# Hyena filter parts made in the feed-forward layer, sums of squares on DVE: one change to a two-layer encoder

## The chip, the core and the metric

The kernel runs on one core of a Trainium2 chip. The metric is the device time of one execution in microseconds (us); three runs of the kernel before took 1322.36, 1323.95 and 1324.27 us, a median of 1323.95. PE is the matrix engine, PEld its weight loads, DVE the vector engine, ACT the scalar engine, POOL the GpSimd engine, SP the engine that only issues DMAs.

## What is computed

Two layers of an encoder over 512 tokens of width 1024. Each layer is a mixer and a convolutional feed-forward block, and each of the four sub-layers is wrapped as `x = x + post_norm(f(pre_norm(x)))` with RMS norms over the width. The mixer of layer 0 joins latent attention and neighbourhood attention; the mixer of layer 1 joins retention and a Hyena operator. What the change touches is the filter of the Hyena operator and the norms:

```python
def rms_norm(x, gain):
    y = x * lax.rsqrt(jnp.mean(x * x, axis=-1, keepdims=True) + EPS)
    return y * gain

def hyena_filters(...):                      # 512 positions, hidden 64, 2 x 512 channels
    h = jnp.sin(freq * (z @ w1 + b1))
    h = jnp.sin(freq * (h @ w2 + b2))
    h = jnp.sin(freq * (h @ w3 + b3))
    h = h @ w4
    return h[:, :512] * window, h[:, 512:] * window

def hyena_operator(...):
    x0, x1, v = split(dwconv3(u_proj, short_conv), 3)
    u = v * x1
    y = irfft(rfft(u, n=1024) * rfft(k_circ, n=1024))[:512] + u * hy_bias
    return y * x0
```

The filter depends on weights alone, not on x.

## The kernel before

Activations lie transposed, width on the partitions: x and the normalised input h are eight tiles of 128x512 (k = 0 to 7). Every large product is made of three fp32r products of parts: `split_to` (line 273) writes hi = fp32r(src) on ACT and lo = src - hi on DVE, and `mm` (line 278) adds hi*hi, hi*lo and lo*hi (lines 280, 281 and 282). Weights are handled the same way in `load_weight` (line 250): the SP queue loads 512 KB into one of two raw buffers, ACT casts it (line 259), DVE subtracts (line 260), three weights ahead of use. PSUM has eight banks under four tags: pj (2), A (3), B (2), C (1).

All instructions are written in one program order; a scheduler orders each engine's instructions ahead of time, by data, buffers and a priority that follows the program, which `high_priority` moves forward and `issue_after` holds back. Each engine, and each queue of DMA issues, then works in that order. A buffer of a phase lies over buffers of the phase before it and waits until those are free.

**The boundary** (line 339) joins a sub-layer to the next one. It makes the last output tiles in two halves of 256 tokens (ca, cb); `evac` squares each; `stats` (line 286) sums over the partitions by products with a column of ones (line 292), a POOL power gives the factor (line 299), `spread` (line 311) makes it a row by transposes (line 316). `update` (line 388) then multiplies f by the factor (line 392), adds the residual x (line 393) and makes h in two parts (`scaled`: ACT line 333, DVE line 334), half by half. `squares` (line 399) squares the new x on ACT (line 406), into the no longer needed old x tiles, and POOL adds them into acc2 (line 407). Meanwhile `proj_halves` (line 455) has PE make the first four products of the next sub-layer, half by half, from weights of which all four are held to the end. Since the new factor is applied after the products, its statistics are needed only then: those of the first half are put behind the third of four product groups, those of the second half behind the fourth (lines 437 to 445). They give rcol and its row Rb.

**The feed-forward block** (line 867) makes 22 pairs of products; each takes PE 2 x 24 products, and DVE and ACT do the rest (lines 894 to 912). In layer 0, at every second pair, one step of `filters` (line 963) runs beside it: three hidden layers (line 975, fp32) with a range-reduced sine, then four token blocks, each with two fp32 products with w4 (line 986), windows, a sum and a difference on POOL (line 989) and their stores of 256 KB (line 990).

**The mixer of layer 1** (line 1047) first writes the eight x tiles to memory (line 1051, ACT's queue) and loads the two DFT constants of 1 MB on POOL's queue (line 934). The four products that the boundary left in PSUM become u: scale by Rb (line 1061), short convolution (lines 1063 to 1065). Products for x1 and x0 follow, between them eight steps of `spectrum` (line 994): a filter tile is loaded (line 1003, ACT's queue), split, and multiplied by the DFT constants into the one bank of tag C. The scale tile cv is a single buffer. `decays` (line 1026) is a chain of some 25 small DVE instructions and one exponential.

Of the kernel before, what the change touches and what calls it, by code (L numbers as in the profile page):

```python
# [16 lines left out]
P = 128  # L17
S = 512
# [187 lines left out]
class Body:  # L206
    def __init__(self, ctx, tc, I, out, dbg=None):
# [10 lines left out]
        self.filt = self.dp.tile([2, S, HC], F32, name="filt")  # L218
# [120 lines left out]
    def boundary(self, pool, tag, x, prod, gpost, gpre, ns, ftag, perm=False, rin=None):  # L339
# [85 lines left out]
        if not last:  # L425
            with self.tc.issue_after(self.pow.ins):
                squares(ca)
# [439 lines left out]
    def ffn(self, p, x, h, pre, l):  # L867
# [15 lines left out]
        if l == 0:  # L883
            new = lambda n, tag, bufs: p.tile([P, S], F32, tag=tag, bufs=bufs, name=self.nm(n))
            room = [new("fa", "s", 3) for _ in range(3)] + [new("fb", "flt", 2) for _ in range(2)]
            steps = self.filters(room + [self.X("fc") for _ in range(2)])

        for j in range(FT):
# [5 lines left out]
            nc.vector.tensor_tensor(t, gps, Rb, ALU.mult)  # L894
# [68 lines left out]
    def filters(self, room):  # L963
        nc = self.nc
        z, fw, w4f, w4b, fh, a, n = room
        w4 = (w4f, w4b)
        nc.sync.dma_start(z[:33], self.I["fz"])
        nc.sync.dma_start(fw[:64, :192], self.I["fw"][:64, :192])
        for d in range(2):
            nc.sync.dma_start(w4[d][:64], self.I["fw"][:64, 192 + d * HC:192 + (d + 1) * HC])  # L970
        yield
        k = 33
        for i in range(3):
# [4 lines left out]
            yield  # L978
        for tk in range(4):
            par, hh = tk // 2, tk % 2  # L980
            lhs = z[:64].rearrange("p (m two) -> p two m", two=2)[:, par, hh * P:hh * P + P]
            win = (a, n)
            for d in range(2):
                nc.sync.dma_start(win[d], self.I["fwin"][:, (tk * 2 + d) * HC:(tk * 2 + d + 1) * HC])
                ps = self.PS("C")
                nc.tensor.matmul(ps, lhs, w4[d][:64], start=True, stop=True)
                nc.vector.tensor_tensor(win[d], ps, win[d], ALU.mult)
            for i, (t, op) in enumerate(((fh, ALU.add), (fw, ALU.subtract))):
                nc.gpsimd.tensor_tensor(t, a, n, op)
                nc.sync.dma_start(self.filt[i, tk * P:(tk + 1) * P], t)  # L990
# [3 lines left out]
    def spectrum(self, mats, at, kt, spec):  # L994
        nc = self.nc
        for par in range(2):
            for trig in range(2):
                m = 2 * par + trig
                sd = []
                for hh in range(2):  # L1000
                    t = self.X("sd", tag="xb")
                    tk = 2 * par + hh
                    nc.scalar.dma_start(t, self.filt[trig, tk * P:(tk + 1) * P])
                    sd.append(at(trig))
                    self.split_to(*sd[-1], t)
                for ft in range(2):
                    ps = self.PS("C")
                    for hh in range(2):
                        c = slice(ft * P, ft * P + P)
                        self.mm(ps, (mats[0][:, m, hh, c], mats[1][:, m, hh, c]), sd[hh], hh == 0, hh == 1)  # L1010
                    if par == 0:
                        t = self.X("sp", tag="xb")
# [270 lines left out]
```

## Time and profile before

| | us |
|---|---|
| median of three runs | 1323.95 |
| the profiled execution, its own time | 1324.02 |
| its span, first to last instruction | 1321.9 |
| PE busy | 1282.6 |
| DVE busy | 809.0 |
| ACT busy | 583.1 |
| POOL busy | 132.5 |

Layer 0's mixer ends near 255 us, the first boundary lies at 255 to 300, layer 0's feed-forward block at 300 to 640, the second boundary and the start of layer 1's mixer at 640 to 720, the third boundary at 935 to 980, layer 1's feed-forward block behind it. Times in the trace count from the span's start. In a timeline a row gives start, duration, engine, line, operation, output and inputs, shape and count, and in brackets how long the engine stood idle before it and for whom. A matmul's duration is its own way through the array; what it costs PE is the distance to the next start.

### The profile page before, as it was taken

Reading aid. Unit: us, or ns where it says so; the run is one execution under the profiler, and the core shown is the slowest. Engines: PE = TensorE matmul, PEld = TensorE weight load, DVE = VectorE, ACT = ScalarE, POOL = GpSimd, SP = SyncE. Lnnn points to the kernel's source line nnn. Section 1 sums busy time; section 2 is a strip of 40 time slices with the busy share of each in tenths; the row PEclk is TensorE's granted clock in tenths of the full one; section 3 lists DMA queues with packets and bytes.
Section 4 is the critical chain, followed back from the end, with each engine's and each line's share of the span. In section 5 each row is a group of like instructions: output and inputs, shape, how many; then the busy total and the mean of one; then the engine's idle time right before and its main releaser. Section 6 shows DMA issues by size and latency. Waiting matters only on the chain.

```text
span 1321.9 us, 16451 instructions
## 1 busy us (share of the span) xinstructions
PE 1282.6 (97%) x6370; PEld 1062.2 (80%) x6370; DVE 809.0 (61%) x1269; ACT 583.1 (44%) x943; POOL 132.5 (10%) x126
## 2 busy tenths in 40 slices
PE   8999799999999999999889999999999999999997
PEld 7788677997877788888887878778988888888886
DVE  7679897479756555222668795775775555553223
ACT  5355798456523333222444234544553333332221
POOL 4021322040011000000230000000210000000002
PEclk9999899999999999999989999999999999999999
DMA  7222012223434322333253233213233333333331
GB/s 269 81 64 80 1 32 81 80 70 118 119 121 144 112 96 96 103 105 103 73 207 127 64 114 107 72 57 115 79 96 100 98 101 101 96 96 97 111 96 64
DMA packets 41402, 130.35 MB, mean 99 GB/s; under 512 B 4619, under 2 KB 6859, under 8 KB 40812
## 3 DMA queue, kind: packets, MB, share of 16 engines
q1 hardware_dynamic: 35708, 116.66, 27.6%
q10 hardware_dynamic: 5040, 8.45, 1.9%
q0 software_dynamic: 576, 4.19, 0.8%
q8 instruction: 50, 0.82, 0.3%
q14 instruction: 28, 0.23, 0.1%
HBM read 122.99 MB, written 6.29 MB: 98 GB/s over the span
## 4 chain that ended last, share of the span: by engine, by line
PE 84%; DVE 7%; ACT 3%; issue 2%; DMA 2%; POOL 1%; SPq 0%; DVEq 0%; ACTq 0%; POOLq 0%
PE pspj L280 16%; PE pspj L282 16%; PE pspj L281 16%; PE psA L280 9%; PE psA L282 9%; PE psA L281 9%; DVE wlo L260 2%; DVE f L393 1%; DVE h L334 1%; ACT e L792 1%; DVE f L392 1%; DMA raw<-in_w 1%; PE psB L292 1%; PE psB L669 1%; PE psB L808 1%
## 5 line engine op out<-in xcount | busy, mean ns | idle before, releaser
L259 ACT CAST whi<-raw 128x1024 fp32r<-128x1024 f32 (+1 forms) x200 | 209.2, 1048 | 437.7 <-PE pspj L281 243.0
L260 DVE TENSOR_TENSOR wlo<-raw,whi 128x1024 fp32r<-128x1024 f32 (+1 forms) x200 | 247.6, 1240 | 215.2 <-ACT whi L259 212.8
L280 PE MATMUL pspj<-h,whi 128*128 128x512 f32 (+1 forms) x664 | 251.8, 379 | 2.4 <-DVE v L597 2.3
L281 PE MATMUL pspj<-h,whi 128*128 128x512 f32 (+1 forms) x664 | 250.9, 378 | 1.4 <-DVE h L334 1.4
L282 PE MATMUL pspj<-h,wlo 128*128 128x512 f32 (+1 forms) x664 | 251.2, 378 | 0.0
L282 PE MATMUL psA<-h,wlo 128*128 128x512 f32 (+1 forms) x424 | 156.3, 369 | 4.4 <-DVE wlo L260 4.3
L280 PE MATMUL psA<-h,whi 128*128 128x512 f32 (+1 forms) x424 | 157.6, 372 | 0.0
L281 PE MATMUL psA<-h,whi 128*128 128x512 f32 (+1 forms) x424 | 155.8, 367 | 0.0
L280 PEld LDWEIGHTS pspj<-h,whi 128*128 128x128 f32 x664 | 126.5, 191 | 25.2 <-DVE v L597 2.7
L281 PEld LDWEIGHTS pspj<-h,whi 128*128 128x128 f32 x664 | 126.5, 191 | 24.0 <-DVE h L334 1.8
L282 PEld LDWEIGHTS pspj<-h,wlo 128*128 128x128 f32 x664 | 126.5, 190 | 22.5 <-issue 0.2
L280 PE MATMUL pspj<-ahi,whi 128*128 128x512 f32 x308 | 121.4, 394 | 0.0
L282 PE MATMUL pspj<-ahi,wlo 128*128 128x512 f32 x308 | 120.7, 392 | 0.0
L281 PE MATMUL pspj<-alo,whi 128*128 128x512 f32 x308 | 119.5, 388 | 0.0
L280 PEld LDWEIGHTS psA<-h,whi 128*128 128x128 f32 x424 | 81.0, 191 | 19.8 <-issue 5.4
L282 PEld LDWEIGHTS psA<-h,wlo 128*128 128x128 f32 x424 | 80.8, 191 | 19.4 <-DVE wlo L260 6.3
L281 PEld LDWEIGHTS psA<-h,whi 128*128 128x128 f32 x424 | 80.9, 191 | 12.2
L299 POOL TENSOR_TENSOR r<-v,mhalf 128x2 f32<-128x2 f32 (+1 forms) x14 | 13.7, 982 | 702.1 <-DVE v L297 543.0
L894 DVE TENSOR_TENSOR t<-psA,Rb 128x512 f32<-128x512 f32 x40 | 27.6, 690 | 87.8 <-PE psA L282 87.7
L282 PEld LDWEIGHTS pspj<-ahi,wlo 128*128 128x128 f32 x308 | 57.8, 188 | 13.6
L281 PEld LDWEIGHTS pspj<-alo,whi 128*128 128x128 f32 x308 | 57.8, 188 | 12.9
L280 PEld LDWEIGHTS pspj<-ahi,whi 128*128 128x128 f32 x308 | 57.9, 188 | 11.5
(357 smaller groups left out, 2188.4 us busy)
## 6 DMA issues: line engine op xcount, KB each, us to landing
raw<-in_w SPq DMA_DIRECT2D x198, 512.0 KB, 3.5
x<-in_xT SPq DMA_DIRECT2D x16, 256.0 KB, 4.2
fc<-in_fwin SPq DMA_DIRECT2D x8, 256.0 KB, 4.0
filt<-fa SPq DMA_DIRECT2D x8, 256.0 KB, 2.0
xspill<-f ACTq DMA_DIRECT2D x8, 256.0 KB, 2.2
sd<-filt ACTq DMA_DIRECT2D x8, 256.0 KB, 3.4
x<-xspill ACTq DMA_DIRECT2D x8, 256.0 KB, 3.0
rpb<-in_rpb SPq DMA_DIRECT2D x4, 384.0 KB, 4.8
```

The lines of the kernel that those rows point to most:

```text
L259: nc.scalar.copy(hi[:, c], raw[:, c])
L260: nc.vector.tensor_tensor(lo[:, c], raw[:, c], hi[:, c].bitcast(F32), ALU.subtract)
L280: nc.tensor.matmul(ps, stat[0], mov[0], start=start, stop=False)
L281: nc.tensor.matmul(ps, stat[0], mov[1], start=False, stop=False)
L282: self.last_mm = nc.tensor.matmul(ps, stat[1], mov[0], start=False, stop=stop).ins
L292: nc.tensor.matmul(ps[:, j:j + 1], a[:, j * P:(j + 1) * P], self.ones, start=a is accs[0], stop=a is accs[-1])
L299: self.pow = nc.gpsimd.tensor_tensor(r, v, self.mhalf[:, :c], ALU.pow)
L334: self.nc.vector.scalar_tensor_tensor(lo, src, g, hi.bitcast(F32), ALU.mult, ALU.subtract)
L392: nc.vector.tensor_tensor(f, f, R, ALU.mult)
L393: (nc.gpsimd if last and k in POOLK else nc.vector).tensor_tensor(v(f), v(f), own(k, cs), ALU.add)
L669: tr = lambda o, i: nc.tensor.transpose(o, i, self.ident)
L894: nc.vector.tensor_tensor(t, gps, Rb, ALU.mult)
```

## The change

Sums of squares: POOL's adds go; after both halves, DVE adds the square tiles 2 to 7 into tile 1 and that into acc2 (seven adds of 128x512). The squares of the first half are no longer held until POOL's power. The statistics of all four column blocks are made at once, after the fourth product group.

Filter: the third hidden layer's output is split, its two parts stacked on 128 partitions, w4 loaded twice and split, so that one fp32r product of 128 rows and one of 64 rows replace one fp32 product. Sum and difference are on DVE; each is split into hi and lo there, and both parts are stored. The spectrum then loads the parts, sixteen loads of 256 KB on POOL's queue behind the constants, all asked for at the start of the mixer, and splits nothing.

Order: the mixer's x0 tiles are allocated ahead of the constants, whose loads get a higher priority; the four finished products are scaled straight into the x0 tiles; the writing of x waits for the second convolution; the decays are computed in layer 0's feed-forward block, at pair 4.

```diff
-        self.filt = self.dp.tile([2, S, HC], F32, name="filt")
+        self.filt = self.dp.tile([2, 2, S, HC], F32, name="filt")
...
                     nc.scalar.activation(own(k, cs), v(f), AF.Square)
-                    nc.gpsimd.tensor_tensor(v(acc2[:, cs]), v(acc2[:, cs]), own(k, cs), ALU.add)
+
+
+        def square_sum():
+            for k in range(2, KT):
+                nc.vector.tensor_tensor(x[1], x[1], x[k], ALU.add)
+            v = v3 if perm else (lambda a: a)
+            nc.vector.tensor_tensor(v(acc2), v(acc2), own(1, slice(0, S)), ALU.add)
...
         if not last:
-            with self.tc.issue_after(self.pow.ins):
-                squares(ca)
+            squares(ca)
...
         squares(cb)
+        square_sum()
         next(g)
         self.new_factor()
-        next(g)
-        with self.tc.issue_after(self.last_mm):
-            r = self.stats([acc2[:, ca]], D, 256, out=self.rcol[:, :2])
         drain(g)
         with self.tc.issue_after(self.last_mm):
-            nc.scalar.copy(self.Rb[:, ca], self.spread(r, "C"))
             with self.tc.high_priority(HP):
-                r = self.stats([acc2[:, cb]], D, 256, out=self.rcol[:, 2:])
-            nc.scalar.copy(self.Rb[:, cb], self.spread(r, "C"))
+                self.stats([acc2], D, out=self.rcol)
+            nc.scalar.copy(self.Rb, self.spread(self.rcol, "C"))
...
-            new = lambda n, tag, bufs: p.tile([P, S], F32, tag=tag, bufs=bufs, name=self.nm(n))
-            room = [new("fa", "s", 3) for _ in range(3)] + [new("fb", "flt", 2) for _ in range(2)]
-            steps = self.filters(room + [self.X("fc") for _ in range(2)])
+            steps = self.filters(lambda tag, bufs, dt=F32: p.tile([P, S], dt, tag=tag, bufs=bufs, name=self.nm("f" + tag)))
...
-            nc.vector.tensor_tensor(t, gps, Rb, ALU.mult)
+            scaled = nc.vector.tensor_tensor(t, gps, Rb, ALU.mult)
+            if l == 0 and j == 4:
+                with self.tc.issue_after(scaled.ins):
+                    self.decay = self.decays(self.cp)
...
-            self.nc.gpsimd.dma_start(t.rearrange("p m a b -> p (m a b)"), self.I[name][:, i * 2048:(i + 1) * 2048])
+            self.consts = self.nc.gpsimd.dma_start(t.rearrange("p m a b -> p (m a b)"), self.I[name][:, i * 2048:(i + 1) * 2048]).ins
...
-    def filters(self, room):
-        nc = self.nc
-        z, fw, w4f, w4b, fh, a, n = room
-        w4 = (w4f, w4b)
+    def filters(self, new):
+        nc = self.nc
+        z, fw, fh = new("s", 3), new("s", 3), new("s", 3)
+        a, n = new("flt", 2), new("flt", 2)
         nc.sync.dma_start(z[:33], self.I["fz"])
         nc.sync.dma_start(fw[:64, :192], self.I["fw"][:64, :192])
-        for d in range(2):
-            nc.sync.dma_start(w4[d][:64], self.I["fw"][:64, 192 + d * HC:192 + (d + 1) * HC])
         yield
...
+
+        zz = self.X("zz", F32R)
+        split = lambda t: t.rearrange("p (two m) -> p two m", two=2)
+        zv = z[:64].rearrange("p (m two) -> p two m", two=2)
+        nc.scalar.copy(split(zz[:64]), zv)
+        nc.vector.tensor_tensor(split(zz[64:]), zv, split(zz[:64].bitcast(F32)), ALU.subtract)
+        w4 = []
+        for d in range(2):
+            raw, hi, lo = self.X("w4"), new("s", 3, F32R), self.X("w4l", F32R)
+            for half in (raw[:64], raw[64:]):
+                nc.sync.dma_start(half, self.I["fw"][:64, 192 + d * HC:192 + (d + 1) * HC])
+            nc.scalar.copy(hi, raw)
+            nc.vector.tensor_tensor(lo[:64], raw[:64], hi[:64].bitcast(F32), ALU.subtract)
+            w4.append((hi, lo))
+        yield
         for tk in range(4):
-            par, hh = tk // 2, tk % 2
-            lhs = z[:64].rearrange("p (m two) -> p two m", two=2)[:, par, hh * P:hh * P + P]
-            win = (a, n)
+            ts = slice(tk * P, tk * P + P)
+            win, t = (a, n), new("s", 3)
             for d in range(2):
                 nc.sync.dma_start(win[d], self.I["fwin"][:, (tk * 2 + d) * HC:(tk * 2 + d + 1) * HC])
                 ps = self.PS("C")
-                nc.tensor.matmul(ps, lhs, w4[d][:64], start=True, stop=True)
+                nc.tensor.matmul(ps, zz[:, ts], w4[d][0], start=True, stop=False)
+                nc.tensor.matmul(ps, zz[:64, ts], w4[d][1][:64], start=False, stop=True)
                 nc.vector.tensor_tensor(win[d], ps, win[d], ALU.mult)
-            for i, (t, op) in enumerate(((fh, ALU.add), (fw, ALU.subtract))):
-                nc.gpsimd.tensor_tensor(t, a, n, op)
-                nc.sync.dma_start(self.filt[i, tk * P:(tk + 1) * P], t)
+            nc.vector.tensor_tensor(t, a, n, ALU.add)
+            nc.vector.tensor_tensor(n, a, n, ALU.subtract)
+            for i, src in enumerate((t, n)):
+                hl = self.X("fh", F32R), self.X("fl", F32R)
+                self.split_to(*hl, src)
+                for part in range(2):
+                    nc.sync.dma_start(self.filt[part, i, ts], hl[part].bitcast(F32))
             yield
...
-        for par in range(2):
-            for trig in range(2):
-                m = 2 * par + trig
-                sd = []
+        parts = []
+        for m in range(4):
+            parts.append([at(m % 2) for _ in range(2)])
+            for hh in range(2):
+                tk = 2 * (m // 2) + hh
+                for part in range(2):
+                    with self.tc.high_priority(300), self.tc.issue_after(self.consts):
+                        nc.gpsimd.dma_start(parts[m][hh][part], self.filt[part, m % 2, tk * P:(tk + 1) * P])
+        yield
+        for m in range(4):
+            par, trig = m // 2, m % 2
+            sd = parts[m]
+            for ft in range(2):
+                ps = self.PS("C")
                 for hh in range(2):
-                    t = self.X("sd", tag="xb")
-                    tk = 2 * par + hh
-                    nc.scalar.dma_start(t, self.filt[trig, tk * P:(tk + 1) * P])
-                    sd.append(at(trig))
-                    self.split_to(*sd[-1], t)
-                for ft in range(2):
-                    ps = self.PS("C")
-                    for hh in range(2):
-                        c = slice(ft * P, ft * P + P)
-                        self.mm(ps, (mats[0][:, m, hh, c], mats[1][:, m, hh, c]), sd[hh], hh == 0, hh == 1)
-                    if par == 0:
...
+                    c = slice(ft * P, ft * P + P)
+                    self.mm(ps, (mats[0][:, m, hh, c], mats[1][:, m, hh, c]), sd[hh], hh == 0, hh == 1)
...
-        for k in range(KT):
-            nc.scalar.dma_start(spill[k * P:(k + 1) * P], x[k])
-        mats = self.dft_consts(p, "dftf")
+        x0 = [p.tile([P, S], F32, name=f"x0{j}") for j in range(4)]
+        with self.tc.high_priority(300):
+            mats = self.dft_consts(p, "dftf")
...
-        def conv(jj, dst):
-            ps = pre[jj - 8] if jj >= 8 else self.proj(h, "A" if jj == 4 else "pj")
-            t = p.tile([P, S], F32, tag="cv", name=self.nm("cv"))
+        def scaled(ps, t):
             nc.vector.tensor_tensor(t, ps, Rb, ALU.mult)
+            return t
+
+        def conv(jj, dst, t=None):
+            if t is None:
+                t = scaled(self.proj(h, "A" if jj == 4 else "pj"), p.tile([P, S], F32, tag="cv", name=self.nm("cv")))
             cw = [self.col(C_SC + i * 12 + jj) for i in range(3)]
-            nc.scalar.activation(dst, t, AF.Copy, scale=cw[1])
...
-        u, x0 = [], [p.tile([P, S], F32, name=f"x0{j}") for j in range(4)]
+        next(steps)
+
         for j in range(4):
-            u.append(conv(8 + j, p.tile([P, S], F32, name=f"u{j}")))
+            scaled(pre[j], x0[j])
+        u = []
+        for j in range(4):
+            u.append(conv(8 + j, p.tile([P, S], F32, name=f"u{j}"), x0[j]))
+            if j == 1:
+                with self.tc.issue_after(self.taken):
+                    for k in range(KT):
+                        nc.scalar.dma_start(spill[k * P:(k + 1) * P], x[k])
         for j in range(4):
             x1 = conv(4 + j, x0[j])
             nc.vector.tensor_tensor(u[j], u[j], x1, ALU.mult)
...
-        lg = self.decays(p)
+        lg = self.decay
```

## Rows read from the trace of the kernel before

**Rows 1.** The page, part 1: busy time, share of the span, instructions.

```profile
PE 1282.6 (97%) x6370; PEld 1062.2 (80%) x6370; DVE 809.0 (61%) x1269; ACT 583.1 (44%) x943; POOL 132.5 (10%) x126
```

**Rows 2.** Stretches: length, busy (instructions) by engine, clock, DMA share, GB/s.

```profile
400.00:420.00 20.00, 20.00 (x82) 14.87 (x82) 11.21 (x17) 6.29 (x8) 0.69 (x1) 1.00 0.38 121
...
650.00:660.00 10.00, 7.38 (x56) 6.57 (x54) 10.00 (x15) 6.21 (x13) 7.25 (x7) 1.00 0.24 71
...
690.00:700.00 10.00, 7.88 (x24) 5.97 (x23) 7.46 (x17) 3.83 (x5) 0.00 (x0) 0.66 0.59 214
```

**Rows 3.** PE's waits, 640 to 720 us: total us, times, longest us.

```profile
PE psC L282 <- DMA dftflo<-in_dftf: 2.1, 1, 2.1
...
PE psA L282 <- DVE wlo L260: 2.0, 1, 2.0
...
PE pspj L281 <- DVE h L334: 1.4, 2, 0.9
...
PE psC L280 <- DMA dftfhi<-in_dftf: 1.3, 1, 1.3
...
PE psB L1087 <- DVE u L1076: 1.3, 1, 1.3
```

**Rows 4.** PE's waits, 255 to 325 us, same columns.

```profile
PE psA L282 <- DVE wlo L260: 1.2, 2, 1.0
```

**Rows 5.** The chain that ended last: start us, us.

```profile
661.38 0.21 PE psA L280
...
666.92 0.21 PE psA L281
...
667.61 0.12 PE psA L280
...
697.12 0.43 PE pspj L281
```

**Rows 6.** Timeline of POOL and DVE, 648 to 661 us: start us, us.

```profile
652.53 6.61 POOL L407 TENSOR_TENSOR acc<-acc,f 128x256 f32<-128x256 f32 x6
...
648.00 0.71 DVE L393 TENSOR_TENSOR f<-f,f 128x256 f32<-128x256 f32 x1
...
650.80 0.50 DVE L334 SCALAR_TENSOR_TENSOR h<-f,cols,h 128x256 fp32r<-128x256 f32 x1
...
656.23 1.08 DVE L334 SCALAR_TENSOR_TENSOR h<-f,cols,h 128x256 fp32r<-128x256 f32 x1
...
658.31 1.29 DVE L393 TENSOR_TENSOR f<-f,f 128x256 f32<-128x256 f32 x1
```

**Rows 7.** Timelines of POOL and PE, last row the chain: the constants' load.

```profile
676.29 0.95 POOL L407 TENSOR_TENSOR acc<-acc,f 128x256 f32<-128x256 f32 x1
...
681.19 0.50 PE L292 MATMUL psB<-ones,acc 128*128 128x1 f32 x4
...
682.31 0.76 POOL L934 DMA_DIRECT2D dftfhi<-in_dftf  x1 [5.08 <-issue]
...
684.84 7.61 DMA dftflo<-in_dftf
```

**Rows 8.** Groups by line and shape: busy us, mean ns, idle before.

```profile
L1181 DVE TENSOR_TENSOR rp<-rp,rp 128x512 f32<-128x512 f32 x8 | 5.5, 682 | 0.0
...
L299 POOL TENSOR_TENSOR r<-v,mhalf 128x4 f32<-128x4 f32 x6 | 7.8, 1294 | 84.4 <-DVE v L295 80.4 <-DVE v L297 4.0
```

**Rows 9.** Timeline of DVE, then the chain, after the first boundary.

```profile
306.17 2.02 DVE L906 TENSOR_TENSOR t<-psA,g 128x512 f32<-128x512 f32 x2
...
307.73 0.23 PE psA L280
```

**Rows 10.** Timeline of PE around one product of the filter's last layer.

```profile
364.23 0.39 PE L282 MATMUL pspj<-h,wlo 128*128 128x512 f32 x1
...
364.54 1.13 PE L986 MATMUL psC<-fa,fb 64*128 64x512 f32 x2
...
365.94 0.40 PE L281 MATMUL psA<-h,whi 128*128 128x512 f32 x1
```

More of the change, by code (lines that the diff above doesn't have):

```diff
@@ L995, in spectrum @@
         nc = self.nc
-        for par in range(2):
-            for trig in range(2):
-                m = 2 * par + trig
-                sd = []
-                for hh in range(2):
-                    t = self.X("sd", tag="xb")
-                    tk = 2 * par + hh
-                    nc.scalar.dma_start(t, self.filt[trig, tk * P:(tk + 1) * P])
-                    sd.append(at(trig))
-                    self.split_to(*sd[-1], t)
-                for ft in range(2):
-                    ps = self.PS("C")
-                    for hh in range(2):
-                        c = slice(ft * P, ft * P + P)
-                        self.mm(ps, (mats[0][:, m, hh, c], mats[1][:, m, hh, c]), sd[hh], hh == 0, hh == 1)
-                    if par == 0:
-                        t = self.X("sp", tag="xb")
-                        nc.scalar.activation(t, ps, AF.Copy, scale=1.0 / 512)
-                        spec[ft, trig] = t
-                    else:
-                        e, o, d = spec[ft, trig], kt(), kt()
-                        nc.vector.scalar_tensor_tensor(o, ps, 1.0 / 512, e, ALU.mult, ALU.add)
-                        if trig == 0:
-                            nc.vector.scalar_tensor_tensor(d, ps, -1.0 / 512, e, ALU.mult, ALU.add)
-                        else:
-                            nc.vector.scalar_tensor_tensor(d, ps, 1.0 / 512, e, ALU.mult, ALU.subtract)
-                        spec[ft, trig] = (o, d)
-                    yield
@@ new lines, in spectrum @@
+        parts = []
[12 more added lines that the diff above has]
+                ps = self.PS("C")
+                for hh in range(2):
+                    c = slice(ft * P, ft * P + P)
+                    self.mm(ps, (mats[0][:, m, hh, c], mats[1][:, m, hh, c]), sd[hh], hh == 0, hh == 1)
+                if par == 0:
+                    t = self.X("sp", tag="xb")
+                    nc.scalar.activation(t, ps, AF.Copy, scale=1.0 / 512)
+                    spec[ft, trig] = t
+                else:
+                    e, o, d = spec[ft, trig], kt(), kt()
+                    nc.vector.scalar_tensor_tensor(o, ps, 1.0 / 512, e, ALU.mult, ALU.add)
+                    if trig == 0:
+                        nc.vector.scalar_tensor_tensor(d, ps, -1.0 / 512, e, ALU.mult, ALU.add)
+                    else:
+                        nc.vector.scalar_tensor_tensor(d, ps, 1.0 / 512, e, ALU.mult, ALU.subtract)
+                    spec[ft, trig] = (o, d)
+                yield
@@ L1049, in mixer1 @@
         spill = self.dp.tile([D, S], F32, name="xspill")
[L1050 to L1052 removed]
+        x0 = [p.tile([P, S], F32, name=f"x0{j}") for j in range(4)]
+        with self.tc.high_priority(300):
+            mats = self.dft_consts(p, "dftf")
         two = lambda tag: tuple(p.tile([P, S], F32R, tag=tag, bufs=8, name=self.nm(tag)) for _ in range(2))
         rcol, Rb = self.rcol, self.Rb
[L1058 to L1060 removed]
+        def scaled(ps, t):
             nc.vector.tensor_tensor(t, ps, Rb, ALU.mult)
+            return t
+        def conv(jj, dst, t=None):
+            if t is None:
+                t = scaled(self.proj(h, "A" if jj == 4 else "pj"), p.tile([P, S], F32, tag="cv", name=self.nm("cv")))
             cw = [self.col(C_SC + i * 12 + jj) for i in range(3)]
[L1063 removed]
+            self.taken = nc.scalar.activation(dst, t, AF.Copy, scale=cw[1]).ins
             nc.vector.scalar_tensor_tensor(dst[:, 1:], t[:, :S - 1], cw[0], dst[:, 1:], ALU.mult, ALU.add)
```

## The prediction

> **What bounds the kernel now.** I read the page first: PE is busy for 97% of the span, DVE for 61%, ACT for 44%; PEld's 80% are weight loads beside PE's products [rows 1]. So a change can win in two ways only: less work on PE, or fewer of PE's gaps and slow stretches. Next I read PE's waits boundary by boundary (a boundary is the stretch in which one layer's output is normalised and becomes the next one's input). There are three with a following layer: 255 to 300, 640 to 720 and 935 to 980 us. The middle one is the bad one. In it PE waits 2.0 us for a weight's low part, 1.4 for input tiles, 1.3 and 2.1 for the two DFT constants, and 1.3 for a u tile further on [rows 3]. The first boundary has 1.2 us, 1.0 in one piece [rows 4]; the third shows that row again, digit for digit.
>
> The waits cost more than they last. Behind the 2.0 us wait, from 661.4 to 666.9 us, 27 products of 256 columns take 0.21 each, and the next ones 0.12; behind the 2.1 us wait, up to 697.5, 12 products of 512 columns take 0.43, against 0.23 elsewhere [rows 5, 9]. The granted clock of 690 to 700 is 0.66 of full, so it was at half rate, 1.2 GHz, in most of that stretch, right after PE had stood still [rows 2].
>
> Why PE stands still there: from 650 to 660 DVE is busy all of the time and PE 7.4 of 10 us [rows 2]. DVE is slow because POOL adds squares beside it. While POOL runs six adds (6.6 us from 652.5), DVE's split of an input tile takes 1.08 us in place of 0.50 and its residual add 1.29 in place of 0.71 [rows 6].
>
> **The change part by part.**
>
> *Sums of squares from POOL to DVE, in all three boundaries.* Removed: 14 POOL adds each, and the rule that ACT's squares of the first half wait for POOL's power; ACT has room, so that alone costs nothing. Added: seven DVE adds of 128x512, behind the last update, about 0.68 us each [rows 8], 4.8 us per boundary. With POOL quiet, the DVE steps of 652 to 660 fall back: three splits lose 0.6, 0.6 and 0.3, three adds 0.1, 0.6 and 0.6, together 2.9 us (two of the six are shown) [rows 6]. The weight's low part, now the cause of the 2.0 us wait, then comes 2.9 us sooner; PE without its 1.4 us of earlier waits asks for it 1.4 sooner. So 3.4 us of waits [rows 3] shrink to about 0.5: gain 2.9. With one short wait left I take the clock to hold: 27 products at 0.12 in place of 0.21 give 2.5 [rows 5]. Together 5.4; bounds 1.5 (half the wait, no clock) and 5.9 (all).
>
> In the first and third boundary the longest wait is 1.0 each [rows 4], behind the same slowed steps; I take 2.0 for both, between 0 and 2.4.
>
> What the adds can delay: the statistics are now one block after the fourth product group, over all four columns. In the middle boundary POOL's last add ended at 677.2 and PE came to the statistics at 681.2 [rows 7], 4.0 us of cover. PE now comes some 5 us sooner, DVE is done with its updates some 3 to 5 us sooner, then adds. The adds of early tiles can run as ACT delivers squares, but the last two cannot, and the last one is a strided one. I charge 0.7 us of PE wait there, between 0 and 4.8. Elsewhere PE has other products to run.
>
> From the statistics on, everything is one column block wider: the power on POOL takes 1.29 us for four columns [rows 8], in place of a narrower one; the transposes and the copy double. So the scale factor comes about 1 us later (bounds 0 and 2). What hides it is the next product group, 24 products of 0.23 us, 5.5 us. At the second step the cover is thin: after the first boundary the two multiplications that free a PSUM buffer end at 307.2 and 308.2, and PE's group that needs the first one starts at 307.7 [rows 9]. One us later costs 0.5; I charge 0.6 for the first and third boundary together.
>
> *Filter's last layer.* Eight fp32 products become sixteen fp32r ones. From the product ahead of one to the second behind it are 365.94 - 364.23 = 1.71 us, of which two normal steps are 0.46; so one fp32 product costs 1.25 us [rows 10], and a pair of fp32r ones 0.46 at the 0.23 of [rows 9]. Gain 8 x 0.79 = 6.3; bounds 4.4 (should a pair cost 0.7, with a gap around it) and 6.3. The three hidden layers stay fp32.
>
> *Filter's parts stored.* Eight splits (ACT and DVE) leave the middle boundary for the feed-forward layer before it, eight POOL adds go to DVE there, the stores double to sixteen of 256 KB, and four loads of the last layer's weights come in place of two. All stand in SP's queue: a store waits there for DVE's split, and the weight loads queued behind it for the store, as they now do for POOL's adds. PE never waits in that stretch, and of 400 to 420 DVE is busy 11.2 of 20 us, ACT 6.3, the DMA engines 0.38 [rows 2]. Per step of 22 us, DVE gets two adds and two splits, 2.7 us. Weights are loaded three ahead, some 16 us of products. I take zero; without that cover a step costs its 2.7 us, 11 in all. The decays (some 25 tiny DVE steps and one ACT table load) go to the same place: zero.
>
> *Constants and loads placed anew.* Now the high part's load waits in POOL's queue until 682.3, one us after PE's statistics of 681.2 [rows 7]: its buffer lies over tiles that include the sum of squares. In the new order four input tiles take that place, and the constants lie over tiles that the down projection frees near 650. They take 7.6 us to land [rows 7], so they are there some 15 us ahead of use. Gone are 1.3 and 2.1 us [rows 3] and the slow stretch behind, 12 x (0.43 - 0.23) = 2.4 [rows 5, 9]: 5.8, bounds 0 and 6. The sixteen filter loads follow in the same queue, 4 MB. The spill of the residual moves behind the second convolution, which takes eight DMA issues off ACT when ACT feeds DVE: counted in the first part. A power on POOL can stand behind one or two of these issues (0.76 us each [rows 7]): inside the bounds.
>
> One constant of 1 MB takes 7.6 us to land while another and weights are under way [rows 7]. The Trainium skill (DMA: Bandwidth & Descriptors, Issuing engines are not separate DMA queues) states that DMAs of all issuing engines run on the same 16 DMA engines and interleave. The row fits that but does not prove it; by the rule alone, moving loads to POOL's queue gains no bandwidth, and 6 MB in one go could go the way of the rival "late loads" (1318), where the sum has 1305.2.
>
> *First products scaled early.* The four finished products leave PSUM one behind another, and DVE has no splits between. Of the 1.3 us that PE waits for a u tile [rows 3] I take half, 0.6; bounds 0 and 1.3.
>
> **Sum.** 5.4 + 2.0 - 0.7 - 0.6 + 6.3 + 5.8 + 0.6 = 18.8 us. The profiled execution took 1324.02 us (span 1321.9), 0.07 above the median of the three runs, so nothing is shifted: 1305.2 us.
>
> **The rivals.**
> *DVE takes back what it won.* The 4.8 us of adds on DVE equal the relief. For: DVE is at 100% in the middle boundary [rows 2]. Against: the adds stand behind the last update. Then only filter, constants and 0.5 remain: 1324.0 - 12.6 = 1311.4. Chance 0.22.
> *Late loads.* The constants again wait for a late release, and 4 MB of filter parts stand behind them. 2 MB took from 682.3 to 692.5, so 1 MB more, what the first spectrum step needs, adds 5 us of wait. Gain 18.8 - 5.8 - 5 - 2.4 for the clock = 5.6: 1318. Against: the first loads' new place. Chance 0.12.
> *Slower: DVE waits for ACT.* POOL's adds never held DVE up. If the seven adds are queued among the updates, each waits at the head of DVE's queue for ACT's square, and tiles for PE behind it. It decides once a boundary loses over 6.3 us (18.8 / 3). At 7 x (0.68 + 0.7), 0.7 for a wait as long as such an add, a boundary loses 9.7, three 29, 10 more than the sum: 1334. Chance 0.07.
> *No change.* The parts in the feed-forward layer take buffers of the tag that its own tiles rotate through; four steps at the 2.7 us above and four slow stretches of 2.5 us each take back 21: 1326. Chance 0.04.
>
> **The numbers.** The forecast has the remaining 0.55. The likeliest time is 1305.2. Its own range is 1299 (all gains whole, no charges) to 1311 (a third of them lost); with "taken back" and "late loads" the range is 1298 to 1318. A measurement of this kernel can tell 0.2%, 2.6 us, from no change. Faster by more: 0.55 + 0.22 + 0.12 = 0.89; within: 0.04; slower: 0.07.
>
> **What would show it.** Right: no POOL adds at line 407, splits of 256 columns at 0.5 us throughout; granted clock 1.00 in the whole middle boundary; constants issued before 655; no wait on them; sixteen filter products at 0.23. Wrong: PE waiting for the sum or for DVE at the statistics; PE waits between 300 and 640; PE waiting for filter parts. The forecast fails if the order of DVE's queue moves updates behind adds.

## The result and the profile after

The changed kernel takes 1309.49 us (median of four runs, 1307.73 to 1311.0) against 1323.15 for the kernel before on the same chip: ratio 0.9898, 95% interval 0.9883 to 0.9913, so 13.7 us or 1.0% faster. The forecast was 1305.2 with a range of 1298 to 1318. The direction holds and the time lies inside the range, 4.3 us above the forecast; some 5 us of the gain of 18.8 did not come. The profiled execution took 1308.93 us (span 1307.2).

Three views of the changed kernel answer to the rows of before. First the page's busy times [rows 1]:

```profile
PE 1273.0 (97%) x6370; PEld 1059.6 (81%) x6370; DVE 814.7 (62%) x1298; ACT 583.9 (45%) x943; POOL 89.1 (7%) x89
```

POOL lost 43 us of work and DVE took on 6. Next the busy times by stretch [rows 2]:

```profile
650.00:660.00 10.00, 9.26 (x78) 9.06 (x77) 10.00 (x23) 6.42 (x15) 4.70 (x10) 1.00 1.07 371
660.00:680.00 20.00, 17.95 (x128) 16.49 (x127) 14.38 (x24) 8.72 (x13) 4.53 (x8) 1.00 0.72 216
680.00:700.00 20.00, 16.72 (x66) 13.61 (x67) 13.88 (x21) 8.06 (x12) 0.00 (x0) 0.83 0.57 203
```

From 650 to 660 DVE is still busy all of the time, but it now works on 23 instructions there and not 15, and PE works 9.3 of the 10 us and not 7.4. (The same work lies 4 us earlier now; from 646 to 656 the figures are 22 and 9.2.) The granted clock is 1.00 until 680 and then falls again: 0.83 of full from 680 to 700. Then PE's waits from 635 to 740 us [rows 3]:

```profile
PE psC L280 <- ACT Rb L447: 5.3, 1, 5.3
PE psA L282 <- DVE wlo L260: 0.7, 1, 0.7
```

All five waits of [rows 3] above 1 us are gone or small: those on input tiles, on both constants and on the u tile do not appear at all. A new one has come that no row of before had: 5.3 us on ACT's copy of the scale factor, Rb. From 255 to 325 us, where [rows 4] had 1.2 us on a weight, 0.4 is left, for POOL's power (rcol).

**Where the new wait comes from.** The chain that ended last in the changed kernel, start and length:

```profile
670.94 1.24 DVE wlo L260
672.20 3.51 DMA raw<-in_w
675.80 1.06 ACT whi L259
676.88 1.24 DVE wlo L260
678.14 3.46 DMA raw<-in_w
681.70 1.04 ACT whi L259
682.74 0.49 ACT Rb L447
683.28 0.79 PE psC L280
```

Read it from below. PE's product into psC waits for ACT's copy of Rb, which empties the only buffer of that tag. ACT works in order, and ahead of the copy stands the cast of a weight (whi). That cast waits for its load, the load for a raw buffer (there are two), the buffer for DVE's low part of the weight before, and so on back to 670.94. The timelines of PE and ACT show how long the copy could have run already:

```profile
677.35 0.60 PE L316 MATMUL psC<-ident,rcol 128*128 128x128 f32 x4
...
683.28 0.79 PE L280 MATMUL psC<-t,dftfhi 128*128 128x512 f32 x1 [5.33 <-ACT Rb L447]
...
686.86 0.46 PE L282 MATMUL pspj<-h,wlo 128*128 128x512 f32 x1
```

```profile
681.70 1.04 ACT L259 CAST whi<-raw 128x1024 fp32r<-128x1024 f32 x1 [2.56 <-DMA raw<-in_w]
682.65 0.58 ACT L447 COPY Rb<-psC 128x512 f32<-128x512 f32 x1
```

The transposes were done by 677.95; the copy began at 682.65. After the stop PE goes on at half rate (1.2 GHz, 0.43 us from product to product): from 683.28 to 686.86 it starts eight products in 3.6 us where 8 x 0.23 = 1.8 is usual. So 1.8 are lost behind the wait, and with its 5.3 that is some 7 us in one place.

**Where the 15 us came from.** Totals of single profiles differ by some us ahead of the first statistics of the first boundary (the first row of L292 lies at 252.9 to 257.4 us in the profiles read here), in a part that the change doesn't touch. So I compare lengths behind that point: A, from there to the first statistics of the middle boundary; B, to that boundary's statistics over all tiles (the last L292 block in it); C, to the end of the span. Each is a difference of starts of L292 rows, or of the span and one.

| profile | A | B | C | A+B+C |
|---|---|---|---|---|
| before | 385.98 | 39.33 | 640.71 | 1066.02 |
| after | 381.46 | 33.06 | 636.33 | 1050.85 |
| after, second profile | 381.48 | 33.03 | 636.59 | 1051.10 |
| sums alone | 384.81 | 33.10 | 635.31 | 1053.22 |
| sums alone, second profile | 384.81 | 33.03 | 639.88 | 1057.72 |
| sums undone | 382.66 | 38.03 | 643.21 | 1063.90 |
| constants alone | 385.98 | 38.08 | 640.19 | 1064.25 |
| constants and factor | 385.97 | 36.58 | 636.93 | 1059.48 |
| factor ahead | 381.53 | 33.02 | 630.38 | 1044.93 |
| 128 rows | 379.89 | 33.05 | 634.84 | 1047.78 |
| both edits | 379.93 | 33.03 | 630.99 | 1043.95 |
| both edits, second profile | 379.94 | 33.01 | 630.78 | 1043.73 |
| two banks | 378.22 | 33.02 | 630.36 | 1041.60 |

The change gains 4.5 in A, 6.3 in B and 4.4 in C: 15.2 between the two profiles, where the medians have 13.7. The forecast had, on the same cut, about 7.0 (filter and first boundary), 4.7 (middle boundary, less the wait for the sum) and 7.1 (constants, u tile, third boundary). Two of the three fell short.

### The profile page after: what moved, and what is told of

It reads as the page before. It is cut to its first block, busy times and chain, and to the rows that moved or that the text cites. A ratio compares the mean times of both kernels' runs of the same rounds, so it can differ in the third digit from the quotient of the medians.

```text
span 1307.2 us, 16449 instructions
## 1 busy us (share of the span) xinstructions
PE 1273.0 (97%) x6370; PEld 1059.6 (81%) x6370; DVE 814.7 (62%) x1298; ACT 583.9 (45%) x943; POOL 89.1 (7%) x89
## 4 chain that ended last, share of the span: by engine, by line
PE 87%; DVE 4%; ACT 4%; issue 3%; DMA 1%; POOL 1%; SPq 0%; DVEq 0%; ACTq 0%; POOLq 0%
PE pspj L280 17%; PE pspj L282 17%; PE pspj L281 17%; PE psA L280 10%; PE psA L282 10%; PE psA L281 10%; DVE wlo L260 1%; ACT e L794 1%; DMA raw<-in_w 1%; PE psB L292 1%; PE psB L671 1%; PE psC L280 1%; PE psB L810 1%; ACT whi L259 1%; PE psC L281 1%
## 5 line engine op out<-in xcount | busy, mean ns | idle before, releaser
L299 POOL TENSOR_TENSOR r<-v,mhalf 128x2 f32<-128x2 f32 (+1 forms) x14 | 13.7, 976 | 847.9 <-DVE v L297 690.2
```

Of the source, the lines that this page charges most:

```text
L299: self.pow = nc.gpsimd.tensor_tensor(r, v, self.mhalf[:, :c], ALU.pow)
```

## Experiments

Each ratio is to runs of the kernel before on the same chip. Its median there was 1319.7, 1322.36 and 1321.27 us in the three groups of runs, so ratios are compared and not microseconds.

**1. The scale factor's copy ahead on ACT.**

```diff
-            with self.tc.high_priority(WP):
+            with self.tc.high_priority(WP), self.tc.issue_after(self.factor) if self.factor else ExitStack():
...
-            nc.scalar.copy(self.Rb, self.spread(self.rcol, "C"))
+            made = nc.scalar.copy(self.Rb, self.spread(self.rcol, "C"))
+        self.factor = made.ins if perm else self.factor
```

In load_weight this puts every later cast behind the copy in ACT's queue, in the middle boundary only.

> The changed kernel with one order altered: in the middle boundary ACT copies the new scale factor (Rb) before it casts the next weights, no longer behind three casts that wait for loads. Theory (the place in ACT's queue is the cost): the copy starts at about 678 in place of 682.65, PE's wait of 5.3 us shrinks to under 1, and the half-rate stretch behind it (about 1.75 us) goes: 6 to 7 us less, about 1303. Rival (the loads themselves are late, crowded by the 6 MB in POOL's queue, so the same weights hold PE a little later): 0 to 2 us less, 1307 to 1309, with PE waiting for whi or wlo between 680 and 700.

Measured: 0.9857 (0.9842 to 0.9871), against 0.9898 for the changed kernel: 0.4%, 5.4 us. Behind the first statistics it is 5.9 us, all of it in C, a little under the 6 to 7 expected. ACT and PE of this kernel:

```profile
675.13 0.58 ACT L446 COPY Rb<-psC 128x512 f32<-128x512 f32 x1 [1.22 <-PE psC L316]
675.61 1.05 ACT L259 CAST whi<-raw 128x1024 fp32r<-128x1024 f32 x1
```

```profile
674.49 0.60 PE L316 MATMUL psC<-ident,rcol 128*128 128x128 f32 x4
675.77 0.50 PE L280 MATMUL psC<-t,dftfhi 128*128 128x512 f32 x1 [0.68 <-ACT Rb L446]
676.10 0.40 PE L281 MATMUL psC<-t,dftfhi 128*128 128x512 f32 x1
```

The wait is 0.7 in place of 5.3 and the products behind it run at 2.4 GHz (granted clock 1.00 from 670 to 700). PE waits for no weight between 680 and 700, so the rival falls: the loads were not late for PE, only for the queue in which the copy stood.

**2. The second filter product over 128 rows.**

```diff
-            nc.vector.tensor_tensor(lo[:64], raw[:64], hi[:64].bitcast(F32), ALU.subtract)
+            nc.vector.tensor_tensor(lo, raw, hi.bitcast(F32), ALU.subtract)
...
-                nc.tensor.matmul(ps, zz[:64, ts], w4[d][1][:64], start=False, stop=True)
+                nc.tensor.matmul(ps, zz[:, ts], w4[d][1], start=False, stop=True)
```

> The changed kernel with the second product of each filter pair over all 128 rows in place of 64 (the low weights now fill 128 rows, so the product of the two low parts is added as well). Theory (a 64-row product among 128-row ones costs some 0.4 us more): a pair costs 0.46, eight pairs give 8 x 0.40 = 3.2 us, about 1306. Rival (the extra lies in the switch to another accumulator or stationary tile, whatever the rows): a pair still costs 0.85, no difference, 1309.

Measured: 0.9906 (0.9893 to 0.992), no difference from the changed kernel that the times can show. The trace can: PE around one pair, first in the changed kernel, then in this one, where the next pair follows too.

```profile
408.83 0.39 PE L282 MATMUL pspj<-h,wlo 128*128 128x512 f32 x1
409.05 0.40 PE L1001 MATMUL psC<-fs,zz 128*128 128x512 f32 x1
409.38 0.50 PE L1002 MATMUL psC<-w4l,zz 64*128 64x512 f32 x1
409.81 0.50 PE L280 MATMUL psA<-h,whi 128*128 128x512 f32 x1
410.14 0.40 PE L281 MATMUL psA<-h,whi 128*128 128x512 f32 x1
```

```profile
409.49 0.39 PE L282 MATMUL pspj<-h,wlo 128*128 128x512 f32 x1
409.72 0.40 PE L1001 MATMUL psC<-fs,zz 128*128 128x512 f32 x1
409.95 0.40 PE L1002 MATMUL psC<-w4l,zz 128*128 128x512 f32 x1
410.20 0.39 PE L280 MATMUL psA<-h,whi 128*128 128x512 f32 x1
410.42 0.39 PE L281 MATMUL psA<-h,whi 128*128 128x512 f32 x1
...
411.66 0.50 PE L1001 MATMUL psC<-fs,zz 128*128 128x512 f32 x1 [0.15 <-DVE fflt L1003]
```

From the product ahead of a pair to the second behind it: 1.31 us in the changed kernel, 0.93 here. Less two usual steps of 0.23 a pair costs 0.85 with 64 rows and 0.47 with 128, so the theory holds for the first pair of each two. The second pair now comes before DVE has emptied psC, the only buffer of its tag: a wait of 0.15, and a slow start around it, make it 0.90. Summed over all of its products, worked out in this way, the filter's last layer takes 10.1 us before, 6.9 after and 5.5 here. A shrinks by 1.57, half of the 3.2 expected; the rest of the 3.1 us in the table is C, where the clock happened to be back sooner (0.91 from 680 to 700, against 0.83). What a 64-row product costs is told by these rows: 0.33 us ahead of it, 0.43 and 0.33 behind it, where 0.23 is usual. The Trainium skill (TensorEngine Tiling (Array Packing), Key Properties) states that changing the tiling mode drains the TensorE; the row fits that, at about 0.4 us for one product of 64 rows among others of 128, if 64 rows count as another mode, which no run here shows. Whether the price lies in the change or in the 64-row product itself was not tried apart.

**3. Another buffer for the second pair**, with both edits above, and both edits without it.

```diff
-                ps = self.PS("C")
+                ps = self.PS("CB"[d])
```

> Both edits together: the scale factor's copy ahead of the weight casts on ACT, and the filter's second products over 128 rows. If the two are independent, from the first statistics to the end 1050.9 - 5.9 - 3.1 = 1041.9 us, and the time 8 to 9 us under the changed kernel's on the same chip. Rival (the scatter of the clock hides the 3 us, as the times of the 128-row kernel alone suggest): 5 to 6 us under.

> The same kernel as in the earlier run of both edits, as the partner of the one with two PSUM buffers on the same chip. Expected: 0.983 to 0.986 of the kernel before, from the first statistics to the end 1043 to 1045 us.

> Both edits together as before (the copy of the scale factor ahead on ACT, the filter's second products over 128 rows), and the second of each two product pairs in a PSUM buffer of another tag, so that it no longer waits for DVE to empty the only one. In the run without this, the first pair of each two cost 0.48 us and the second 0.90, with 0.15 of wait in front of it. Theory (the one buffer is what is left of the pair's cost): all eight cost about 0.47, 1.7 us less between the first statistics and those of the middle boundary (378.3 in place of 379.9). Rival (a pair that follows another within 2 us costs 0.9 by itself): no difference there.

Both edits: 0.9845 (0.9828 to 0.9861) and on another chip 0.9853 (0.983 to 0.9875); behind the first statistics 1044, not the 1041.9 expected, since the 128 rows are worth 1.6 and not 3.1. On its chip it is 6.8 us under the changed kernel (1302.01 against 1308.81), less than the 8 to 9 of two independent gains and a little more than the 5 to 6 of the rival. With the second buffer 0.9835 (0.9814 to 0.9857), 1299.08 us, the fastest kernel of this study. All four products of a step now run through:

```profile
384.46 0.39 PE L282 MATMUL pspj<-h,wlo 128*128 128x512 f32 x1
384.68 0.40 PE L1001 MATMUL psC<-fs,zz 128*128 128x512 f32 x1
384.92 0.40 PE L1002 MATMUL psC<-w4l,zz 128*128 128x512 f32 x1
385.16 0.39 PE L1001 MATMUL psB<-fs,zz 128*128 128x512 f32 x1
385.39 0.39 PE L1002 MATMUL psB<-w4l,zz 128*128 128x512 f32 x1
385.62 0.40 PE L280 MATMUL psA<-h,whi 128*128 128x512 f32 x1
```

Two pairs cost 0.95 together, eight 3.8, and A falls by 1.7 to 378.2, as the theory had it. That is the 6.3 us that the forecast promised for the filter (10.1 - 3.8): its price per pair was right for a pair that neither changes the rows nor waits for its buffer. The times of this and the run beside it overlap; the 1.7 us are read from the trace alone.

**4. The sums of squares alone, and undone.** Alone: the kernel before with the changed boundary (square_sum on DVE, one statistics block, squares free to run early) and nothing else. Undone: the changed kernel with the boundary of before, the same lines turned round. Of the first:

```diff
-                    nc.gpsimd.tensor_tensor(v(acc2[:, cs]), v(acc2[:, cs]), own(k, cs), ALU.add)
...
+        square_sum()
...
-        with self.tc.issue_after(self.last_mm):
-            r = self.stats([acc2[:, ca]], D, 256, out=self.rcol[:, :2])
...
+                self.stats([acc2], D, out=self.rcol)
```

> The kernel before with the boundary of the changed one and nothing else: sums of squares on DVE, statistics as one block. Theory (POOL's adds beside DVE were the middle boundary's loss): statistics of the middle boundary 6 us sooner as in the changed kernel, splits of 256 columns back to 0.5 us, the first and third boundary 0.9 and 1.1 us shorter: 6 to 8 us less, 1315 to 1317. The constants stay as late as before, so PE's waits on them stay, 3.4 us or more. Rival (the gain comes from the filter's splits and loads having left the stretch, not from POOL's adds): under 3 us less, over 1320.

> The kernel before with only the boundary of the changed one, once more, because its nine times lay between 1307.9 and 1317.5 us and its profile was of the fastest. Theory (a PE wait of 2.4 us drops the clock in some runs and not in others): ratio 0.995 to 0.997 again, and a second profile either with the granted clock under 0.9 in 680 to 700 and 3 to 6 us more between the first statistics and the end than the 1053.2 of the first, or again without it. Rival (the scatter lies ahead of the first statistics alone): 1053 us behind that point whatever the total.

> The changed kernel with the boundary of the kernel before put back: squares added by POOL half by half beside DVE's updates, two statistics blocks; filter and constants as changed. Theory: the middle boundary's statistics come 6 us later, splits of 256 columns take up to 1 us again while POOL adds, the wlo waits of 1.0 us return in the first and third boundary: 8 to 10 us more than the changed kernel, less what the wait for the scale factor gives back (up to 5). Rival (POOL's adds matter only together with the filter's splits, which have left the stretch): under 3 us more.

Alone: 0.9954 (0.9936 to 0.9972) and 0.9945 (0.9926 to 0.9964), 6 to 7 us of the change's 13.7. B falls by 6.2, all that it falls in the changed kernel, A by 1.2. That rules out the filter's splits as the cause. The same split on DVE, in the kernel with the sums alone and in the one with the sums undone:

```profile
649.57 0.48 DVE L334 SCALAR_TENSOR_TENSOR h<-f,cols,h 128x256 fp32r<-128x256 f32 x1
```

```profile
651.39 1.12 DVE L334 SCALAR_TENSOR_TENSOR h<-f,cols,h 128x256 fp32r<-128x256 f32 x1
```

With POOL's adds back DVE's splits double again, as in [rows 6], and only beside the adds: in the kernel before, a split at 662.00 us, between two runs of adds, takes 0.47, and one at 670.72, beside the next run, 1.19. The edit's other two parts, one statistics block and the freed squares, were not run apart from the adds; these rows are what speaks for the adds. Not all of B's 6.3 is theirs directly. In the kernel before the clock fell behind the wait for the weight (granted 0.66 from 660 to 670). In the kernel of experiment 5 with the copy ahead, which has the same adds, it held behind a like wait (1.94 us), and B is 36.58, only 3.5 above the changed kernel's; undone, B is 5.0 above it. So the slow steps and their waits are worth 3.5, and the clock the rest, when it falls.

Undone: 0.9989 (0.9976 to 1.0003), 12 us worse than the changed kernel and more than the 8 to 10 expected. Of that C has 6.9, because of a wait that neither kernel has:

```profile
691.10 0.53 POOL L1021 DMA_DIRECT2D t<-filt  x1
691.64 0.72 POOL L299 TENSOR_TENSOR rcol<-v,mhalf 128x2 f32<-128x2 f32 x1
```

```profile
692.42 0.69 PE L316 MATMUL psC<-ident,rcol 128*128 128x128 f32 x2 [8.38 <-POOL rcol L299]
```

While POOL adds until 674.1, the constants and all sixteen filter loads queue behind the adds, and the second half's power behind the loads. So the loads can stand in POOL's queue only because the adds have left it: the parts of the change are not independent.

The two profiles of the sums alone also settle a point on the clock. PE waits for the late constant as before, in both about equally long. The first profile, then the second:

```profile
682.21 0.50 PE L282 MATMUL psC<-t,dftflo 128*128 128x512 f32 x1 [2.42 <-DMA dftflo<-in_dftf]
682.54 0.39 PE L280 MATMUL psC<-t,dftfhi 128*128 128x512 f32 x1
```

```profile
683.05 0.80 PE L282 MATMUL psC<-t,dftflo 128*128 128x512 f32 x1 [2.28 <-DMA dftflo<-in_dftf]
683.64 0.63 PE L280 MATMUL psC<-t,dftfhi 128*128 128x512 f32 x1
```

After 2.42 us PE went on at 2.4 GHz; after 2.28 us it went on at 1.2 (granted clock of 680 to 700: 1.00 and 0.83), and C is 4.6 us longer. So the rival that put all scatter ahead of the first statistics is wrong: what follows such a wait makes up 4.6 of the 5.5 us between these two profiles. That it makes up the whole scatter of this kernel's runs, 1307.9 to 1317.5 us, is not shown.

**5. The constants alone, and with the copy ahead.** Into the kernel before, in mixer1:

```diff
-        mats = self.dft_consts(p, "dftf")
+        x0 = [p.tile([P, S], F32, name=f"x0{j}") for j in range(4)]
+        with self.tc.high_priority(300):
+            mats = self.dft_consts(p, "dftf")
```

The second kernel also puts ACT's second copy of Rb ahead of the two casts that follow the statistics.

> The kernel before with the four input tiles put in the place of the constants' buffers and the constants' two loads given priority, nothing else. In POOL's queue they still stand behind the last add of squares, so they are issued near 677 and not near 649. Theory (the loads' late release was the wait): they land 5 us sooner, the waits of 1.3 and 2.1 us go and with them the slow stretch of 2.4: 3 to 6 us less, 1318 to 1321. Rival (whatever comes after takes the wait over: the copy of the scale factor, which in this order stands behind a weight's cast on ACT): 0 to 2 us less, 1322 to 1324.

> The kernel before with the constants placed early, as in the run of that alone, and ACT's second copy of the scale factor put ahead of the two weight casts that had stood before it (691.31 there, 3.1 us after it could have run). Theory (the constants' gain was real but passed on to that copy): PE's wait of 3.6 us for Rb falls under 1 and the half-rate stretch behind it goes: 4 to 6 us less than the kernel before. Rival (early constants are worth nothing, something else than the copy takes the wait over, the weights whose casts are now behind): 0 to 2 us less, with a PE wait of 2 us or more on whi, wlo or a cv tile between 685 and 700.

Alone: 0.9999 (0.9987 to 1.0011), nothing, as the rival had it. With the copy ahead: 0.9969 (0.9955 to 0.9983), 4.1 us. PE's waits from 635 to 740 us, first of the constants alone:

```profile
PE psC L280 <- ACT Rb L445: 3.6, 1, 3.6
```

and of the kernel with the copy ahead:

```profile
PE pspj L280 <- DVE cv L1061: 2.3, 1, 2.3
...
PE psC L280 <- ACT Rb L445: 0.5, 1, 0.5
```

Early constants take away both waits for them, but ACT's copy, which had been hidden behind those waits, takes over 3.6 us. With the copy ahead the gain appears, less a wait of 2.3 us for the first scaled product that then shows itself, one of those that the rival named. In the two profiles C, where the copy stands, is 3.3 us shorter than with the constants alone; another 1.5 lie in B, where the clock held, and no edit bears on that. The same thing, then, in both kernels: the early loads are worth nothing until ACT's order lets them be. That the copy alone, without early loads, gains nothing was not run; the kernel before speaks for it, since its copy began at 687.18 and PE stood waiting for the constants' low part until 692.49.

**6. The changed kernel again.**

> The changed kernel once more, unaltered, beside the others on one chip, to see how far runs of one kernel scatter. Expected: the ratio to the kernel before within its first interval, 0.988 to 0.991. From the first statistics of the first boundary (L292) to the end of the span 1050 to 1052 us, as in its first profile (1050.85), and the wait of 5.3 us for the copy of the scale factor again; what differs between runs is expected ahead of that point and in which stretch behind a wait the clock is at half rate.

Measured: 0.9899 (0.9884 to 0.9913). The wait is 5.3 us again and the table's row repeats to 0.25 us.

## Why the forecast held in sign and missed in size

Of the signs of being right, no adds at line 407, splits at 0.5, early constants and no wait on them came; a clock of 1.00 in the whole middle boundary and sixteen filter products at 0.23 did not. None of the signs of being wrong came. By parts, behind the first statistics of the first boundary, the sums of squares gave 1.6 more than forecast in the middle boundary and 0.9 more in the two others, the filter 3.0 less, constants and u tile 3.1 less. That the misses partly cancel is luck.

*Sums of squares, middle boundary* (5.4 less 0.7): right in mechanism, measured 6.3, of which 3.5 come also where the clock does not fall (experiment 4); the forecast had 2.9 and 2.5 for the clock. DVE's splits are at 0.47 to 0.53 throughout, and the clock held up to 680. The 0.7 for a wait on the sum was not needed: DVE's last add ends at 670.0, PE comes at 670.9.

```profile
668.89 1.13 DVE L413 TENSOR_TENSOR acc<-acc,f 128x512 f32<-128x512 f32 x1
...
670.87 0.95 PE L292 MATMUL psB<-ones,acc 128*128 128x1 f32 x8
```

The cover is 0.9 us, so the charge was close to becoming real. Two of the adds ran ahead of the last split (at 663.30 and 664.85) and held up nothing, so the rival "DVE waits for ACT" did not come either. The rival "DVE takes back what it won" gave 1311.4, close to the 1309.5 measured, yet nothing of its mechanism is in the trace. A fitting time is no evidence for a mechanism.

*First and third boundary* (2.0 less 0.6): right in mechanism and 0.9 too small, measured 1.2 in A with the sums alone, and 1.1 in the third (L292 rows 932.78 and 1303.78 before, 919.28 and 1289.16 after).

*Filter's last layer* (6.3): mis-sized, measured 3.3 in A. The step that failed is "a pair of fp32r ones 0.46 at the 0.23 of [rows 9]": those products have 128 rows, the second of each pair has 64. Its lower bound, 4.4 for a pair at 0.7 with a gap around it, was still too high; the pair cost 0.85 to 0.88.

*Parts stored, decays* (zero): right, no PE wait between 325 and 635.

*Constants, and the u tile* (5.8 and 0.6): the waits named are all gone, the constants were issued at 648.5 and 649.2 as forecast, and the u tile's wait has left too. What failed is the sentence on the path ahead of them: "So the scale factor comes about 1 us later (bounds 0 and 2)", with the next product group as cover. In the kernel before, which copies in two halves, the second copy began 6.0 us behind its statistics of 681.19:

```profile
687.18 0.37 ACT L445 COPY Rb<-psC 128x256 f32<-128x256 f32 x1
```

In the changed kernel it began 11.8 us behind them (682.65 against 670.87), so 5.8 later and not 1, and 4.7 later than it could. The cover was already used up, because the step priced the copy and did not ask what stands ahead of it in ACT's queue. C gained 4.4, of which 1.1 is the third boundary: 3.3 where 6.4 was forecast. Experiment 1 gives back 5.9 with the copy moved, so 9.2 in all, 2.8 more than the 6.4; where that surplus comes from was not followed up, beyond that about 1 us of C's gain lies in the rest of the mixer.

*Late loads* (the rival at 1318): did not come. The 6 MB went out in one go, the stretch of 650 to 660 has 371 GB/s and a DMA share of 1.07 (packets are counted where they start, so a share can pass 1), and no wait on them followed. The profile page's list of DMA issues, the last column the median us from issue to landing:

```profile
raw<-in_w SPq DMA_DIRECT2D x198, 512.0 KB, 3.5
...
t<-filt POOLq DMA_DIRECT2D x16, 256.0 KB, 7.3
...
dftflo<-in_dftf POOLq DMA_DIRECT2D x1, 1024.0 KB, 7.6
```

The constant's low part took 7.6 in both kernels. The filter's parts take 7.3, against 3.4 for 256 KB loads of the filter before, which ACT's queue issued. The weights' median of 3.5, the same before, is over the whole kernel and says nothing of this stretch: the one weight asked for beside the parts (at 653.62) took 6.5 us to land, where the loads at 672.20 and 678.14 took 3.5. So the crowding had a price, but nobody was waiting: ACT's next casts came from 669.87 on, once PE had freed their buffers, and the parts had landed by 669.9, while the first product with one of them came at 683.28. The Trainium skill (DMA: Bandwidth & Descriptors, Issuing engines are not separate DMA queues) states that DMAs of all issuing engines run on the same 16 engines; the 6.5 of a weight from SP's queue beside loads from POOL's fits that. The rival's own sum takes the clock's 2.4 off twice, once within the 5.8; without that it comes to 1316.

*The range.* The low end of 1299, "all gains whole, no charges", does not come out of the terms: their upper bounds add up to 21.9, which is 1302.

## What to carry to other kernels

When a wait is to be removed, list what stands in the queue of each engine that feeds the next step, and ask which of it waits for something else: a short copy behind a cast that waits for a load costs the load's time, whatever the copy takes. A gain in front of such a copy shows only when the copy is moved too, so a part that is worth nothing alone may pay with its partner: nothing and 4.1 us in experiment 5. And take the price of an operation from a row of the same shape in all dimensions, rows as well as columns.

## What the runs showed of the hardware that was not expected

- One product of 64 rows among products of 128 costs about 0.4 us more than a product of 128 rows with the same 512 columns: 1.31 against 0.93 us across the pair.
- A wait of nearly the same length (2.42 and 2.28 us, at the same instruction of the same kernel) left the clock at 2.4 GHz in one execution and at 1.2 GHz in another. It was the same with a wait of 1.97 us in the kernel before (granted 0.66 from 660 to 670) and one of 1.94 us for the same weight in that with constants and factor (1.00). The price of a stall of this length is therefore a chance and not a number; behind the 5.3 us wait the clock fell in all three profiles that have it. The four runs of experiment 1, without such a stall, lie within 1299.7 to 1302.6 us, the first nine of the sums alone, with one, between 1307.9 and 1317.5; but five runs of both edits, without one, lie between 1299.3 and 1304.2, so the stall is not the only source of scatter.
- Between 650 and 660 us DMA moved 371 GB/s beside a fully busy DVE, and DVE's steps kept their times (0.47 to 0.53 us a split).
